# Twenty-three Strassen pairs instead of twenty-two, and a new order of visits, in a weight-gradient matmul

## The chip, the cores and the metric

The kernel runs on one core of a Trainium2 chip. The time is device microseconds of one execution; the figure for a kernel is the median of several runs. A profile is one execution taken by the hardware profiler, and its times run from the start of its own span.

The engines have short names in the profile: PE is TensorE, which multiplies matrices, and PEld its loading of weights; DVE is VectorE; ACT is ScalarE; POOL is GpSimd, which here only issues loads; SP is SyncE, which issues stores. SBUF is the on-chip memory, PSUM the small memory into which TensorE writes, in eight banks.

## What is computed

```python
batch, m, k, n = 16, 512, 1024, 768
grad_weight = np.einsum('bmk,bmn->kn', input, grad_output)   # float32
```

The batch and the rows of a batch are summed over alike, so this is one product: the transpose of an 8192 x 1024 matrix X with an 8192 x 768 matrix G. The output is 1024 x 768.

## The kernel before

**Blocks and units.** The 8192 rows are cut into 64 blocks of 128 rows. Two blocks make a unit, 32 units in all. Loads convert from float32 to bf16 on the way. The output has four quarters: A (left columns of X, left columns of G), B (left, right), C (right, left) and D (right, right), each 512 x 384. A quarter is four tiles of 128 x 384, one PSUM bank each. So an item costs TensorE four matmuls per product, with 128 x 128 weights from X and 384 moving columns from G.

**Plain items and pairs.** `LOADS` has a letter for each unit. "s" makes two plain items: each of A, B, C and D gets one product from each block, 4 x 4 x 2 = 32 matmuls per unit. "P" makes one pair: the two blocks count as a 2 x 2 arrangement, and Strassen's scheme takes seven products in place of eight, 28 matmuls. Two of the seven are summed straight into A and D; five go into sums of their own, called m, n, o, p and q. The price is six additions on VectorE per pair, three on G and three on X (`sum_g1` to `sum_g3`, `sum_x1` to `sum_x3`, lines 132 to 155). `sum_g3` and `sum_x3` change the loaded block in place. At the end m to q are added to or subtracted from A to D by `share` (line 190), in the order of `SHARES`: t1 stands for the tile rows of A and B that take m and o, l1 for those of C and D, and so on.

**Visits.** PSUM has eight banks, hence room for two of the nine sums at a time (two slots of four banks). `ORDER` is a list of visits, written out by hand. `A17:4!2,1,1,1` reads: go to sum A and multiply all its items up to number 17; `:4` says how many of the four banks ScalarE carries; `!` says that the sum is closed at the end of the visit, and the four numbers how many VectorE fillers (pair sums first, then shares) stand ahead of each bank's eviction. A number ahead of the letter (`5D23`) is how many fillers stand ahead of the visit. A sum is summed on through several visits as long as it stays open.

**What opening and closing cost.** When a sum is closed, each bank is evicted to its accumulator in SBUF (`acc` for A to D, `macc` for m to q). ScalarE evicts the last so many banks by a plain copy (line 300) and must then reload them from SBUF at the next opening (line 267) before TensorE adds on; VectorE evicts the others by adding the bank to the accumulator (line 304, or a copy at line 302 the first time), with no reload. `C20:0+n` opens C from n's accumulator in place of its own (line 274; with a minus sign, line 272), and `share` then leaves that part out.

**Queues.** PE, DVE, ACT and POOL each run their instructions in the order in which the code emits them. POOL issues all loads at the start of its list: for units 2 to 31 first G, then X (lines 107 and 108), held back only by buffers (14 pairs) and by the eight loads that may be in flight. The first blocks come in float32 over SP and ACT, in halves, and are cast by VectorE and ScalarE (`round_by`, lines 210 to 216 and 361 to 367). The last visit has its last tile split into 256 and 128 columns, so that its store can start sooner (lines 329 to 347).

Of the kernel before, what the change touches and what calls it, by code (L numbers as in the profile page):

```python
# [8 lines left out]

P = 128  # L10

LOADS = "ssssssssPPPPPPPPPPPPPPPPPPPPPPss"

ORDER = (
    "C1:4!0,0,0,0 A1 D2:3!0,0,0,0 A2!0,0,0,0 B2:1 C3:3 C4!0,0,0,0 B4!0,0,0,0 A3 A4!0,0,0,0 D4 "
    "B6:3!0,0,0,0 D6 C6:1 C8!0,0,0,0 A8!0,0,0,0 D8 B7:2!0,0,0,0 D10!0,0,0,0 B10:2!0,0,0,0 "
    "A10!0,0,0,0 B12:2!0,0,0,0 C10 A12 A14!0,0,0,0 D14:2!0,0,0,0 C16!0,2,1,1 B16:4!1,0,1,1 D16 "
    "A17:4!2,1,1,1 q2:3!0,1,1,1 m2:3!0,0,0,0 D17 p3:3!2,0,1,1 D18!0,0,0,0 n3:4!0,0,0,2 o3:4 "  # L20
    "3A20:3!3,0,0,1 o4 q5:3!2,0,1,2 m5!0,0,0,0 o6!1,1,0,1 n6!1,0,0,0 p6:4 D20:3 D21 5D23 "
    "3p8!1,1,1,0 A24:2!1,0,1,1 m8:1 2m9!1,0,0,0 D25!0,0,0,1 o9 2o10!2,0,0,0 q9:4 q10!3,1,0,0 "
    "p11!1,0,0,0 n11:4 5o12:4!3,0,1,0 m12:1 n12!5,0,0,0 m13!0,0,0,0 A27 q13:4!4,0,2,0 A30!1,0,0,1 "
    "D29:3 p12:4 1p15 D30 6p16!2,1,0,0 D31!0,0,0,1 o16!2,0,1,0 n17:3!0,1,2,2 m16 A32:3!4,0,0,1 "
    "m18!0,0,0,0 q18 4D35:4!3,0,2,1 q20!0,0,0,0 p19:3 o17:4 3p21 o21 6o22!2,1,0,0 p22!0,0,0,0 A36 "
    "q22:4!3,1,0,1 1A39 m22:4!1,1,1,1 A40 n22:3!1,2,0,1 A42!2,0,0,0 C20:0+n!0,0,0,1 B20:4!0,1,2,2 "
    "D42!2,0,0,0 "
).split()


SHARES = (
    "l20 l21 l22 l23 t20 t21 t22 t23 t10 t11 t12 t13 t30 t31 t32 t33 l10 l11 l12 l13 l30 l31 l32 "
    "l33 "
).split()

WARMUP = [512] * 10 + [128] * 2
# [7 lines left out]
def kernel(  # L44
# [55 lines left out]
    xg = []  # L100
    for u, kind in enumerate(LOADS):
        pool = pairs if u else head
# [299 lines left out]
```

## Time and profile before

| | |
|---|---|
| time, median of 3 runs | 164.0 us (163.97 to 164.2) |
| profiled execution | 164.11 us, span 162.3 us |
| TensorE clock granted | 1.00 |
| PE, PEld busy | 158.0, 93.6 us |
| DVE, ACT, POOL busy | 134.1, 96.4, 34.7 us |
| moved by DMA | 33.4 MB |

A line of the groups or of the timeline reads: line in the code, engine, operation, output <- input, shape, count, then busy time, the mean of one, and idle time of the engine ahead of it with what ended it. In the timeline the first two numbers are start and length of a run of like instructions. An instruction on VectorE or ScalarE overlaps the next one by a little, so the distance of starts, not the length of one, says what it costs in a row.

### The profile page before, as it was taken

What the parts mean: (1) busy time and instruction counts of PE and PEld (TensorE: products, weight loads), DVE (VectorE), ACT (ScalarE), POOL (GpSimd) and SP (SyncE); (2) the same over time, 40 slices, a digit from 0 to 9 for tenths busy, and PEclk for the clock granted to TensorE, in tenths of its full rate; (3) what the DMA queues carried; (4) which work ended last, traced back from release to release, by engine and by line L of the source; (5) the groups of instructions that cost most, each with busy time, mean ns of one, the idle gap of its engine ahead of it and who ended that gap; (6) DMA issues with size and microseconds to landing.
All of it is one profiled execution on the core that took longest, in us unless ns stands there. A gap on an engine that the chain in (4) does not pass through costs nothing.

```text
span 162.3 us, 2773 instructions
## 1 busy us (share of the span) xinstructions
PE 158.0 (97%) x955; PEld 93.6 (58%) x955; DVE 134.1 (83%) x276; ACT 96.4 (59%) x225; POOL 34.7 (21%) x69
## 2 busy tenths in 40 slices
PE   8999999999999999999999999999999999999992
PEld 2456556665666665665665666666666666666661
DVE  0467367945978999998899999989999979999982
ACT  3764716415388667735475779809573907987620
POOL 7442222222222221222222222222212100000000
PEclk9999999999999999999999999999999999999999
DMA  5999999999999999999999999999999999800974
GB/s 170 293 213 213 212 212 216 214 212 212 214 213 213 212 212 214 212 211 213 212 213 217 211 213 215 212 211 216 211 212 214 211 212 212 172 4 2 346 276 156
DMA packets 12398, 33.40 MB, mean 206 GB/s; under 512 B 1376, under 2 KB 4192, under 8 KB 12384
## 3 DMA queue, kind: packets, MB, share of 16 engines
q0 software_dynamic: 9360, 28.64, 89.2%
q1 hardware_dynamic: 2592, 3.47, 6.1%
q10 hardware_dynamic: 432, 1.11, 1.9%
q8 instruction: 7, 0.11, 0.3%
q14 instruction: 7, 0.06, 0.1%
HBM read 58.72 MB, written 3.15 MB: 381 GB/s over the span
## 4 chain that ended last, share of the span: by engine, by line
PE 92%; DMA 4%; DVE 1%; issue 1%; ACT 0%; ACTq 0%; POOLq 0%
PE bank L286 92%; DMA gp<-in_grad_output_dram 4%; PE bank L337 0%; DVE acc L345 0%; DVE acc L304 0%; ACT bank L267 0%; ACTq L267 0%; POOLq L386 0%
## 5 line engine op out<-in xcount | busy, mean ns | idle before, releaser
L286 PEld LDWEIGHTS <-xp 128*128 128x128 bf16 x665 | 64.9, 98 | 44.6 <-issue 0.7
L286 PE MATMUL bank<-gp,xp 128*128 128x384 bf16 x492 | 85.2, 327 | 0.4 <-ACT bank L267 0.2
L300 ACT COPY macc<-bank 128x384 f32<-128x384 f32 x67 | 29.1, 494 | 27.6 <-PE bank L286 27.2
L304 DVE TENSOR_TENSOR acc<-bank,acc 128x384 f32<-128x384 f32 x62 | 31.5, 550 | 12.7 <-PE bank L286 12.2
L286 PEld LDWEIGHTS <-xe 128*128 128x128 bf16 x264 | 25.8, 98 | 17.1
L300 ACT COPY acc<-bank 128x384 f32<-128x384 f32 x53 | 23.5, 486 | 19.0 <-PE bank L286 18.7
L286 PE MATMUL bank<-ge,xp 128*128 128x384 bf16 x173 | 32.1, 326 | 0.0
L286 PE MATMUL bank<-gp,xe 128*128 128x384 bf16 x176 | 30.8, 326 | 0.0
L108 POOL DMA_DIRECT2D xp<-in_input_dram x30 | 15.9, 530 | 52.6 <-DMA xp<-in_input_dram 30.4
L267 ACT COPY bank<-acc 128x384 f32<-128x384 f32 x45 | 20.3, 487 | 8.9 <-DVE acc L304 7.9
L107 POOL DMA_DIRECT2D gp<-in_grad_output_dram x30 | 16.0, 532 | 38.1 <-DMA gp<-in_grad_output_dram 21.0
L267 ACT COPY bank<-macc 128x384 f32<-128x384 f32 x50 | 21.9, 515 | 0.1
L304 DVE TENSOR_TENSOR macc<-bank,macc 128x384 f32<-128x384 f32 x38 | 19.0, 550 | 1.3 <-PE bank L286 1.2
L146 DVE TENSOR_TENSOR xe<-xp 128x1024 bf16<-128x1024 bf16 x22 | 15.0, 684 | 2.8 <-DMA xp<-in_input_dram 2.8
L190 DVE TENSOR_TENSOR acc<-acc,macc 128x768 f32<-128x768 f32 (+1 forms) x24 | 16.4, 750 | 0.1
L286 PE MATMUL bank<-ge,xe 128*128 128x384 bf16 x88 | 15.6, 326 | 0.0
L155 DVE TENSOR_TENSOR xp<-xp 128x1024 bf16<-128x1024 bf16 x22 | 15.0, 682 | 0.0
L132 DVE TENSOR_TENSOR ge<-gp 128x768 bf16<-128x768 bf16 x22 | 12.1, 550 | 0.3 <-DMA gp<-in_grad_output_dram 0.2
L141 DVE TENSOR_TENSOR gp<-gp 128x768 bf16<-128x768 bf16 x22 | 12.1, 549 | 0.0
L150 DVE TENSOR_TENSOR xe<-xp 128x512 bf16<-128x512 bf16 x22 | 9.2, 416 | 0.0
L136 DVE TENSOR_TENSOR ge<-gp 128x384 bf16<-128x384 bf16 x22 | 7.7, 349 | 0.0
L90 PE MATMUL bank<-const-bfloat16-1.0 128*128 128x512 bf16 (+1 forms) x12 | 4.6, 577 | 0.8 <-PEq L386 0.8
(19 smaller groups left out, 20.7 us busy)
## 6 DMA issues: line engine op xcount, KB each, us to landing
xp<-in_input_dram POOLq DMA_DIRECT2D x30, 512.0 KB, 16.8
gp<-in_grad_output_dram POOLq DMA_DIRECT2D x30, 384.0 KB, 16.7
out_dram<-acc SPq DMA_DIRECT2D x15, 192.0 KB, 2.1
xf<-in_input_dram ACTq DMA_DIRECT2D x2, 512.0 KB, 5.1
gp<-in_grad_output_dram POOLq DMA_DIRECT2D x3, 192.0 KB, 6.7
xp<-in_input_dram POOLq DMA_DIRECT2D x2, 256.0 KB, 8.0
gf<-in_grad_output_dram SPq DMA_DIRECT2D x2, 192.0 KB, 4.5
out_dram<-acc SPq DMA_DIRECT2D x1, 128.0 KB, 1.7
```

Source lines behind the costliest of these rows:

```text
L107: nc.gpsimd.dma_start(out=gp, in_=G[rows, :].rearrange("(p m) n -> p m n", m=2))
L108: nc.gpsimd.dma_start(out=xp, in_=X[rows, :].rearrange("(p m) k -> p m k", m=2))
L132: nc.vector.tensor_add(out=ge[:, 0:2, :], in0=g[:, :, 0, :], in1=g[:, :, 1, :])
L141: nc.vector.tensor_sub(out=g[:, 1:3, :], in0=g[:, 1:3, :], in1=g[:, 3::-3, :])
L146: nc.vector.tensor_add(out=xe[:, 0:2, :].rearrange("p a k -> p (a k)"), in0=xp[:, 0, :], in1=xp[:, 1, :])
L150: nc.vector.tensor_add(out=extra[i][0][:, 2, :], in0=xp[:, 0, 0:KH], in1=xp[:, 1, KH:K])
L155: nc.vector.tensor_sub(out=x[:, 1:3, :], in0=x[:, 1:3, :], in1=x[:, 0::3, :])
L190: op(out=dst, in0=dst, in1=src)
L267: nc.scalar.copy(out=bank, in_=sum_of(p, q))
L286: nc.tensor.matmul(bank, stat, mov, start=opening and j == 0 and not carried, stop=close and j == len(items_now) - 1, skip_group_check=car ...
L300: nc.scalar.copy(out=dst, in_=bank)
L304: nc.vector.tensor_add(out=dst, in0=bank, in1=dst)
```

## The change

Unit 7 becomes a pair: fourteen plain blocks at the front and four at the end remain around 23 pairs. The last four names of t3, `t30` to `t33`, leave `SHARES`, whose order changes too; the sum q enters A by opening it, negated (`A34:0-q`). And `ORDER` is a new list: it starts with A, D, C and B, and ends with a visit to D of the same length as before. Nothing else in the code changes; its lines stand one higher.

```diff
-LOADS = "ssssssssPPPPPPPPPPPPPPPPPPPPPPss"
+LOADS = "sssssssPPPPPPPPPPPPPPPPPPPPPPPss"
 ORDER = (
-    "C1:4!0,0,0,0 A1 D2:3!0,0,0,0 A2!0,0,0,0 B2:1 C3:3 C4!0,0,0,0 B4!0,0,0,0 A3 A4!0,0,0,0 D4 "
-    "B6:3!0,0,0,0 D6 C6:1 C8!0,0,0,0 A8!0,0,0,0 D8 B7:2!0,0,0,0 D10!0,0,0,0 B10:2!0,0,0,0 "
-    "A10!0,0,0,0 B12:2!0,0,0,0 C10 A12 A14!0,0,0,0 D14:2!0,0,0,0 C16!0,2,1,1 B16:4!1,0,1,1 D16 "
...
-    "q22:4!3,1,0,1 1A39 m22:4!1,1,1,1 A40 n22:3!1,2,0,1 A42!2,0,0,0 C20:0+n!0,0,0,1 B20:4!0,1,2,2 "
-    "D42!2,0,0,0 "
+    "A1:3!0,0,0,0 D1:1 C2:4!0,0,0,0 B2:2!0,0,0,0 D3!0,0,0,0 A2 B4:1!0,0,0,0 A3 C4:2!0,0,0,0 "
+    "A4!0,0,0,0 D5 D6!0,0,0,0 C6 B5 B6 B7 B8 C8!0,0,0,0 A8:1!0,0,0,0 D10:2!0,0,0,0 B10!0,0,0,0 "
+    "A10:4 A12!0,0,0,0 C11!0,0,0,0 B14:2!0,2,0,0 C14:1!0,0,0,0 2D14:2 2A15:2!3,0,0,1 o2:4!2,0,0,0 "
...
+    "p8 A20:4 3A22!3,0,1,0 p9!1,0,0,1 m9:3 D23:4!0,2,2,1 q10!1,0,1,0 m10 4o10:4 m11!0,1,0,0 "
...
+    "8q18!0,0,0,1 o18 n16:4 4n19!0,2,0,3 D32 o20!1,0,1,1 D33 q20:2!1,0,0,0 D34!1,0,0,2 1m20:2 "
+    "p17:4 m21!4,0,0,0 1p20 p22 3q22:2 3p23!2,0,0,0 q23!0,0,0,0 o23!0,0,0,0 A34:0-q m23:4!4,1,0,0 "
+    "A37 n23:4!0,3,1,0 A41!1,0,1,0 C15:0+p C18!0,1,0,0 B18:4!0,0,1,2 D41!4,0,1,0 "
 ).split()
 SHARES = (
-    "l20 l21 l22 l23 t20 t21 t22 t23 t10 t11 t12 t13 t30 t31 t32 t33 l10 l11 l12 l13 l30 l31 l32 "
-    "l33 "
+    "t20 t21 t22 t23 t10 t11 t12 t13 l10 l11 l12 l13 l20 l21 l22 l23 l30 l31 l32 l33 "
 ).split()
```

## The prediction

> **What bounds the kernel now.** I read the busy shares and slices first, then the chain of waits, then the groups by line, then the timelines of TensorE, ScalarE and VectorE.
>
> ```profile
> PE 158.0 (97%) x955; PEld 93.6 (58%) x955; DVE 134.1 (83%) x276; ACT 96.4 (59%) x225; POOL 34.7 (21%) x69
> ...
> PE   8999999999999999999999999999999999999992
> ...
> DVE  0467367945978999998899999989999979999982
> ...
> DMA  5999999999999999999999999999999999800974
> ...
> PE 92%; DMA 4%; DVE 1%; issue 1%; ACT 0%; ACTq 0%; POOLq 0%
> ...
> L286 PE MATMUL bank<-gp,xp 128*128 128x384 bf16 x492 | 85.2, 327 | 0.4 <-ACT bank L267 0.2
> ```
>
> TensorE is the bound: 92% of the chain is L286. "327" is the latency of a matmul, not its price. The price is the distance of starts, from its timeline:
>
> ```profile
> 34.74 3.09 PE L286 MATMUL bank<-gp,xp 128*128 128x384 bf16 x18
> 38.01 7.31 PE L286 MATMUL bank<-gp,xp 128*128 128x384 bf16 x44 [0.18 <-ACT bank L267]
> ...
> 56.85 2.11 PE L286 MATMUL bank<-gp,xp 128*128 128x384 bf16 x12
> 58.80 2.11 PE L286 MATMUL bank<-ge,xp 128*128 128x384 bf16 x12
> ```
>
> Twelve matmuls take 58.80 - 56.85 = 1.95 us, so 162.5 ns each. The kernel has 929 at L286 and 7 whole ones' worth at L337: 936 x 0.1625 = 152.1 us. The first starts at 5.50, so without a wait the stream would end near 157.6; it ends near 159.05 by starts. Only some 1.4 us is idle or slow: about 0.45 in the first four, which start 0.3 us apart, 0.29 before the tenth (the second block's landing at 7.67), 0.17 at 20.7 (a landing), and 0.35 in the lines above: the eighteenth starts at 34.74 + 17 x 0.1625 = 37.50, the next at 38.01. There ScalarE started a reload 0.38 us after VectorE released it (the wait at L267 below). The rest is under 0.2 us.
>
> VectorE is the second. A pair's six sums cost the distance between the first sums of two pairs with nothing between them, 93.90 - 91.15 = 2.75 us; an eviction of four in 1.94 us costs (1.94 - 0.55)/3, or 0.47 us:
>
> ```profile
> 37.47 0.90 ACT L267 COPY bank<-acc 128x384 f32<-128x384 f32 x2 [4.22 <-DVE acc L304]
> ...
> 68.09 1.94 DVE L304 TENSOR_TENSOR macc<-bank,macc 128x384 f32<-128x384 f32 x4
> ...
> 91.15 0.55 DVE L132 TENSOR_TENSOR ge<-gp 128x768 bf16<-128x768 bf16 x1
> ...
> 93.90 0.55 DVE L132 TENSOR_TENSOR ge<-gp 128x768 bf16<-128x768 bf16 x1
> ```
>
> The DMA row is full until 140 us because loads run ahead on their own pace (one unit per 4.3 us); TensorE is stopped by a landing only at the two places named.
>
> **What the Trainium skill says.** "TensorE: Matmul & The Clock Gate", section "Wait — 56ns, not 53.3ns?", gives warm starts N/2.4 + 2.5 ns apart: 162.5 ns for 384 columns, exactly what the trace has. Its section "What's actually happening" says the array runs at half rate until it has been busy for some 3.4 us; the first four matmuls, 0.3 us apart, agree. "VectorE: DVE Perf Modes", section "The perf-mode tier table (the rule you actually need)", has tensor_tensor at twice the rate for bf16 in SBUF and at single rate with PSUM: here 768 bf16 take 550 ns and 384 f32 from PSUM take 550 ns too. So evictions cannot be had cheaper by moving them about on VectorE.
>
> **The change part by part.** Counts are from the two instruction orders.
>
> (1) Unit 7 becomes a pair: 28 matmuls instead of 32. **-4 x 0.1625 = -0.65 us** on TensorE, all of it on the path. VectorE gains 2.75 us of sums and may start them when unit 7 lands (36.3 us) rather than unit 8 (40.6).
>
> (2) Shares: the four one-sided subtractions t3 go (4 x 0.47 = -1.9 us on VectorE). In their place A34 opens its banks with the negated q by four ScalarE multiplies at L272. Not seen in the trace; at least a plain copy L274 (0.41 us apart), at most twice that. They fall at 136 to 138 us, beside o23's twelve matmuls (1.95 us) on the other banks: 0 on the path, at most 0.3.
>
> (3) Order: VectorE's evictions rise from 111 to 122 (+11 x 0.47 = +5.2 us). ScalarE's fall from 120 to 117 and its reloads and openings from 99 to 98: about -1.5 us. VectorE in sum +2.75 - 1.9 + 5.2 = **+6.0 us**. That is not on the path while sums stay ahead of use. Before, from 40.7 to 135.5, VectorE has 22 x 2.75 + 56 x 0.47 = 86.8 us in 94.8. After, from 36.3 to about 135.5 (the last pair's landing at 133.9 is the same) it has 23 x 2.75 + 68 x 0.47 = 95.2 in 99.2. Its slack falls from 8.0 to 4.0 us.
>
> (4) Start: A1, D1, C2 instead of C1, A1, D2. A1 needs the columns cast first, so it can start at 5.3, not 5.5. D1 needs the right half of the first gradient block, which is cast from 6.46 to 6.82. Four matmuls, a wait, four more end at 7.5; in both orders the tenth waits for 7.67. **0**, between -0.05 and +0.2.
>
> (5) Loads and end: POOL issues the same 65 DMAs in the same order, SP and ACT the same loads and stores, the last visit is again seven items with a split last bank. **0**; a pair buffer freed late would have to be late by more than the 16.7 us that a load is in flight. The 3.1 us from last matmul to end stay.
>
> (6) Waits that go and come. The 0.35 at 37.5 belongs to D14's reload, released late by an A14 eviction; that pair of visits is gone. How far the late start of ScalarE would recur I cannot see: 0 to -0.35, I take -0.2. New waits, worked on the same clock (7.72 us at the tenth matmul, 0.1625 each): A10:4 is matmul 144, wanted at 29.9 after 0.2 of earlier waits. Its bank 3 was left by D10 at 28.7, ScalarE evicts it from 28.8 and reloads four banks from 29.2 every 0.413, ready at 29.75, 30.16, 30.57 and 30.99; a two-item visit takes a bank every 0.325, at 29.87, 30.20, 30.52 and 30.85. Wait 0.14. The same sum gives 0.15 at A20:4, 0.17 at C4:2 and some 0.1 at q20:2. Sums: 8q18 is matmul 656, reached at 113.6. VectorE must have done 17 pairs (46.7), four sums of the 18th (1.8) and 55 evictions (25.8), 74.3 us from 36.3: ready at 110.6 plus its own waits. In the whole stretch before, those on TensorE were 2.7 us and those on landings 3.0. So ready about 113.3 to 114: some 0.1 here and 0.1 at 4n19. Together **+0.6**, less 0.15 for the small waits of before that go with their visits: +0.45. Bounds: 0 if each reload starts a little earlier than I reckon, +1.2 if VectorE is 1 us later.
>
> Sum: -0.65 - 0.2 + 0.45 = **-0.4 us**. The profiled execution took 164.1, the median of three is 164.0 (163.97 to 164.2). 164.0 - 0.4 = **163.6**. Less than 0.2% (0.33 us) is about what this measurement can't tell from no change.
>
> **The rivals.**
> Full gain: both kinds of waits vanish: -0.65 - 0.2: 163.15. For it: searched margins could be as wide as 0.1 us. Against it: every two-item visit with four reloads loses 3 x 0.088 us unless it starts ahead. Chance 0.10.
> New waits eat it: +0.7 to +0.9 of waits against -0.65 and no gain from the old: 164.0 to 164.2. For it: evictions in all rise from 231 to 239, each a bank to be emptied in time. 0.23. This is also the case in which the change doesn't do what it says, a longer lead.
> Slower: VectorE becomes the bound between 60 and 120 us. Its in-order queue mixes sums with evictions that wait on TensorE; when these waits exceed the 2.9 us that I allow up to matmul 656, each further microsecond delays the sums, and TensorE by as much. Waits of 4.1 us (half again the old 2.7) give 1.2. With -0.65, -0.2 and +0.25 for the reloads that is +0.6, so 164.6; from 3.5 us on it is slower than before. For it: slack halved. Against it: VectorE, running behind the landings, no longer waits for them. 0.17.
>
> **How the numbers follow.** The forecast -0.4 has 0.50, its own range 163.3 to 163.95. Faster by over 0.2%: 0.40 of the forecast's case and the full gain's 0.10: 0.50. Within: 0.10 of the first and 0.20 of the second rival: 0.30. Slower: 0.03 of the second and 0.17 of the third: 0.20. The range 163.2 to 164.5 leaves out about half the full gain and over half the slower case, some 0.15.
>
> **What would show it.** Right: 925 matmuls at L285, starts still 162.5 ns apart, the wait of 0.2 us near 38 us gone, small waits on ScalarE's bank reloads at 14-16, 30-31 and 72 us, VectorE's busy sum near 140 us, and the last matmul near 158.8. Wrong: VectorE waiting less than 2 us between 36 and 113 us (then the full gain), or waits of TensorE's weight loads on xe, xp or of its matmuls on ge by over 0.5 us together (then the third rival); a clock below 1.0 or loads ending later than 142.5 would upset all of it.

## The result, and the profile after

The changed kernel takes **163.57 us** (median of 6 runs, 163.39 to 163.7), the kernel before 163.99 (6 runs, 163.84 to 164.2): ratio **0.9972**, 95% interval 0.9959 to 0.9985. The profiled execution took 163.7 us, its span 161.9 (before 162.3), at a granted clock of 1.00. The gain is 0.42 us, and the changed kernel has four matmuls less (x951 in place of x955), which are worth 0.65.

The page of the changed kernel, with the rows that were shown of before:

```profile
PE 157.1 (97%) x951; PEld 92.7 (57%) x951; DVE 139.6 (86%) x289; ACT 94.6 (58%) x221; POOL 34.6 (21%) x69
...
PE   8799999999999999999999999999999999999992
...
DVE  0557947469979999999989999999998999999992
...
DMA  5999999999999999999999999999999999902675
...
PE 93%; DMA 3%; DVE 1%; SPq 0%; issue 0%
...
L285 PE MATMUL bank<-gp,xp 128*128 128x384 bf16 x468 | 80.9, 326 | 1.0 <-DVE gp L206 1.0
```

TensorE is the bound as before, and VectorE is busier by 5.5 us. New are the 7 in the second slice of PE and, in the last row, one idle time of 1.0 us, ended by VectorE's cast of gp (L206). The chain of waits of the changed kernel tells the same (start, length, what):

```profile
1.17 5.52 DMA gf<-in_grad_output_dram
...
6.71 0.37 DVE gp L206
...
7.12 150.51 PE bank L285 x921
157.64 0.78 PE bank L336 x7
```

Once TensorE has the cast half block at 7.12, it is a single piece to the end. In the chain of before it starts at 7.72, after a landing, and is broken twice, by a landing at 20.75 and by the late reload at 38.01:

```profile
1.23 6.45 DMA gp<-in_grad_output_dram
...
7.72 13.03 PE bank L286 x79
...
38.01 120.05 PE bank L286 x737
```

"One piece" doesn't mean that nothing waits: the chain doesn't break for waits below some 0.1 us. I took them from the timeline of TensorE, as the distance of two starts beyond 162.5 ns. The lines of the changed kernel that hold such a wait:

```profile
7.12 35.12 PE L285 MATMUL bank<-gp,xp 128*128 128x384 bf16 x214 [0.96 <-DVE gp L206]
...
71.09 2.89 PE L285 MATMUL bank<-ge,xp 128*128 128x384 bf16 x16
...
74.46 2.81 PE L285 MATMUL bank<-ge,xe 128*128 128x384 bf16 x16
...
112.27 2.87 PE L285 MATMUL bank<-gp,xe 128*128 128x384 bf16 x16
...
115.63 4.79 PE L285 MATMUL bank<-gp,xe 128*128 128x384 bf16 x28
```

Sixteen matmuls without a wait take 15 x 0.1625 + 0.33 = 2.76 us, 28 take 4.71 and 214 take 34.94. So these lines hold 0.18, 0.13, 0.05, 0.11 and 0.08 us. From the tenth matmul to the last, all such waits sum to:

| | before | changed |
|---|---|---|
| start of the tenth matmul | 7.72 | 7.93 |
| waits after it | 0.68 | 0.69 |
| start of the last matmul | 158.99 | 158.58 |

So the account of these two executions is **-0.65 for the four matmuls, +0.21 for a later start, +0.02 for the waits: -0.42 us**. The 0.68 of before are a landing (0.17 at 20.4 us), the late reload (0.345 at 37.5) and small ones. The 0.69 after are all small: 0.066 at 15.1 us (C4), 0.13 at 30.4 to 30.8 (A10), 0.063 at 43.7 (X of unit 8, landed at 43.89), 0.13 at 71.6 to 71.9 (A20), 0.045 and 0.054 at 75.0 and 84.1, 0.097 at 113.6 (8q18), 0.065 at 118.4 (4n19), 0.013 at 124.3 (q20), and 0.03 in single hundredths.

### The profile page after: what moved, and what is told of

Same layout as the page of the kernel before. It is cut to its first block, busy times and chain, and to the rows that moved or that the text cites. A ratio compares the mean times of both kernels' runs of the same rounds, so it can differ in the third digit from the quotient of the medians.

```text
span 161.9 us, 2755 instructions
## 1 busy us (share of the span) xinstructions
PE 157.1 (97%) x951; PEld 92.7 (57%) x951; DVE 139.6 (86%) x289; ACT 94.6 (58%) x221; POOL 34.6 (21%) x69
## 4 chain that ended last, share of the span: by engine, by line
PE 93%; DMA 3%; DVE 1%; SPq 0%; issue 0%
PE bank L285 93%; DMA gf<-in_grad_output_dram 3%; PE bank L336 0%; DVE acc L344 0%; SPq L81 0%; DVE gp L206 0%
## 5 line engine op out<-in xcount | busy, mean ns | idle before, releaser
L285 PEld LDWEIGHTS <-xp 128*128 128x128 bf16 x649 | 63.3, 98 | 43.6 <-issue 1.5
L285 PE MATMUL bank<-gp,xp 128*128 128x384 bf16 x468 | 80.9, 326 | 1.0 <-DVE gp L206 1.0
L299 ACT COPY macc<-bank 128x384 f32<-128x384 f32 x73 | 31.5, 493 | 25.0 <-PE bank L285 24.9
L303 DVE TENSOR_TENSOR acc<-bank,acc 128x384 f32<-128x384 f32 x69 | 34.7, 551 | 8.7 <-PE bank L285 8.3
L285 PE MATMUL bank<-gp,xe 128*128 128x384 bf16 x184 | 32.4, 326 | 0.0
L266 ACT COPY bank<-macc 128x384 f32<-128x384 f32 x56 | 25.3, 503 | 8.0 <-DVE macc L303 6.9
L299 ACT COPY acc<-bank 128x384 f32<-128x384 f32 x44 | 19.5, 486 | 15.4 <-PE bank L285 15.3
L107 POOL DMA_DIRECT2D xp<-in_input_dram x30 | 15.9, 530 | 53.1 <-DMA xp<-in_input_dram 29.8
L106 POOL DMA_DIRECT2D gp<-in_grad_output_dram x30 | 15.9, 531 | 37.5 <-DMA gp<-in_grad_output_dram 14.8
L303 DVE TENSOR_TENSOR macc<-bank,macc 128x384 f32<-128x384 f32 x44 | 22.5, 552 | 1.5 <-PE bank L285 1.2
L266 ACT COPY bank<-acc 128x384 f32<-128x384 f32 x34 | 15.2, 492 | 8.6 <-DVE acc L303 8.5
L189 DVE TENSOR_TENSOR acc<-acc,macc 128x768 f32<-128x768 f32 (+1 forms) x20 | 14.6, 791 | 0.0
```

Source lines behind the costliest of these rows:

```text
L106: nc.gpsimd.dma_start(out=gp, in_=G[rows, :].rearrange("(p m) n -> p m n", m=2))
L107: nc.gpsimd.dma_start(out=xp, in_=X[rows, :].rearrange("(p m) k -> p m k", m=2))
L189: op(out=dst, in0=dst, in1=src)
L266: nc.scalar.copy(out=bank, in_=sum_of(p, q))
L285: nc.tensor.matmul(bank, stat, mov, start=opening and j == 0 and not carried, stop=close and j == len(items_now) - 1, skip_group_check=car ...
L299: nc.scalar.copy(out=dst, in_=bank)
```

## The experiments

Each asks what decides one term of that account. Ratios are against runs of the kernel before on the same chip in the same session; the chip is not the same in all sections. The theory that I held is the prediction's: fewer matmuls, less a few small waits at places that can be named, VectorE behind but not the bound.

### The changed kernel again

The same code a second time, to see what in the profile is the kernel's and what is one execution's.

> The changed kernel itself, as the yardstick for the others on the same chip. Its trace gave the account to be tested: four matmuls fewer -0.65 us, the start +0.21 (fifth matmul at 7.12 because the right half of the first gradient block landed at 6.69), waits after the tenth matmul 0.70 before and 0.69 now. If the start's wait is a landing that jumps about, the landing lies between 6.4 and 6.7 and the time at 163.4 to 163.7, 0.3 to 0.6 us under before.

Measured: 163.54 us (163.43 to 165.12, 8 runs, seven of them below 163.71), before 163.95; ratio 0.9987 with an interval of 0.9965 to 1.001, which has the one run of 165.12 in it. The half block of G whose cast opened TensorE at 6.71 in the first profile landed earlier here. VectorE's and TensorE's timelines of this run:

```profile
6.25 0.35 DVE L206 CAST gp<-gf 128x384 bf16<-128x384 f32 x1
```

```profile
6.65 3.60 PE L285 MATMUL bank<-gp,xp 128*128 128x384 bf16 x20 [0.37 <-DVE gp L206]
```

The fifth matmul starts at 6.65 in place of 7.12, the tenth at 7.65 in place of 7.93: the start costs nothing this time. The data lay there at 5.97 (I had expected 6.4 to 6.7), and the cast waited only for an eviction ahead of it on VectorE. So the loss at the start is that of one landing, which came at 5.97 once and at 6.69 once.

But 0.17 of the 0.28 us gained are lost again at matmul 62, in the visit D5, which wants X of unit 2. From the timeline of the weight loads of this run:

```profile
16.32 1.74 PEld L285 LDWEIGHTS <-xp 128*128 128x128 bf16 x12 [0.39 <-DMA xp<-in_input_dram]
```

That load landed at 16.29 here. In the first profile it was there at 16.24, and TensorE, late from the start, came only at 16.45. The same wait, 0.17 to 0.20 us, stands in the profiles of four edits below (A10, A20, the six additions, the second sums). So the new order wants this landing before it comes, and a late start hides it: the term of the start and that of the waits are not independent. The waits after the tenth matmul sum to 0.83 here; those at 30, 71.6, 84, 113.6 and 118.4 us return.

### The pairs without the new order

Twenty-three pairs with the order of before, its items numbered anew and six fillers set ahead of C14:

```diff
-    "A1:3!0,0,0,0 D1:1 C2:4!0,0,0,0 B2:2!0,0,0,0 D3!0,0,0,0 A2 B4:1!0,0,0,0 A3 C4:2!0,0,0,0 "
+    "C1:4!0,0,0,0 A1 D2:3!0,0,0,0 A2!0,0,0,0 B2:1 C3:3 C4!0,0,0,0 B4!0,0,0,0 A3 A4!0,0,0,0 D4 "
...
+    "A10!0,0,0,0 B12:2!0,0,0,0 C10 A12 A14!0,0,0,0 D14:2!0,0,0,0 6C14!0,2,1,1 B14:4!1,0,1,1 D15 "
+    "A16:4!2,1,1,1 q3:3!0,1,1,1 m3:3!0,0,0,0 D16 p4:3!2,0,1,1 D17!0,0,0,0 n4:4!0,0,0,2 o4:4 "
...
```

> Twenty-three pairs visited in the old order: the same visits with items renumbered, six fillers more ahead of C14, old shares. Theory 1 (the pair's 0.65 us is only to be had with an order that leaves VectorE room): VectorE gets 2.75 us of sums more with its old slack of 8 us spread in the wrong places, and TensorE waits on sums or reloads by some 2 us more: slower than before by 1 to 2.5 us, about 165.5. Rival (the pair brings the gain, the order is neutral): 163.4, and no waits on VectorE.

Measured: **166.2 us** (165.88 to 166.47), ratio 1.0131, interval 1.0115 to 1.0146. The 0.65 us of the extra pair are gone, and over 2 us on top. TensorE's timeline of this run where it happens:

```profile
43.23 0.49 PE L286 MATMUL bank<-ge,xp 128*128 128x384 bf16 x2
43.90 0.32 PE L286 MATMUL bank<-ge,xp 128*128 128x384 bf16 x1 [0.17 <-DVE acc L304]
44.96 0.48 PE L286 MATMUL bank<-ge,xp 128*128 128x384 bf16 x2 [0.74 <-DVE acc L304]
45.90 1.31 PE L286 MATMUL bank<-ge,xp 128*128 128x384 bf16 x7 [0.45 <-DVE xp L155]
...
48.47 1.80 PE L286 MATMUL bank<-gp,xe 128*128 128x384 bf16 x10 [0.93 <-DVE xe L146]
```

Four waits, 2.97 us in all between 40 and 60 us; in the 102 us from 60 to 162 only 0.13. TensorE waits for evictions (acc L304) and for sums (xp L155, xe L146) by turns. The queue of VectorE in this run shows why:

```profile
40.56 0.68 DVE L155 TENSOR_TENSOR xp<-xp 128x1024 bf16<-128x1024 bf16 x1
41.16 0.55 DVE L304 TENSOR_TENSOR acc<-bank,acc 128x384 f32<-128x384 f32 x1
41.63 0.55 DVE L132 TENSOR_TENSOR ge<-gp 128x768 bf16<-128x768 bf16 x1
...
42.36 0.55 DVE L304 TENSOR_TENSOR acc<-bank,acc 128x384 f32<-128x384 f32 x1
...
45.16 0.68 DVE L155 TENSOR_TENSOR xp<-xp 128x1024 bf16<-128x1024 bf16 x1
...
47.72 0.69 DVE L146 TENSOR_TENSOR xe<-xp 128x1024 bf16<-128x1024 bf16 x1 [0.67 <-DMA xp<-in_input_dram]
```

Up to 47 us it works back to back, and C14's evictions stand behind one or two sums each: D15, which takes over C14's banks, gets them only when sums that are wanted later are done. The third wait is for the last sum of the second pair (unit 8). The fourth and longest, 1.10 us, is for the first X sum of the third pair, and there VectorE itself waited: X of unit 9 landed at 47.70. So this order asks for unit 9 before it is loaded.

The changed kernel doesn't come to the pairs later. From its TensorE and VectorE timelines:

```profile
42.09 0.33 PE L285 MATMUL bank<-ge,xp 128*128 128x384 bf16 x1
...
48.98 2.11 PE L285 MATMUL bank<-gp,xe 128*128 128x384 bf16 x12
```

```profile
44.86 0.68 DVE L154 TENSOR_TENSOR xp<-xp 128x1024 bf16<-128x1024 bf16 x1
```

Its first product of a pair is in A15, at matmul 219 (42.09 us); with the old order it is D15, at matmul 225 (43.23). The last sum of the second pair is done at 45.54, against 45.84 here. What differs is what TensorE wants next. The old order wants that last sum at matmul 230, in A16, and unit 9 at matmul 239, in q3; with twenty-two pairs the same visits come to unit 9 only at matmul 262, for a plain unit 7 has 32 matmuls there and a pair only the 8 of A and D. In the same way only B14's 8 matmuls lie between C14's end and D15, where there were 16. The new order sets o2, m2, D15, n2 and D16, products of the first two pairs, ahead of q3, and comes to unit 9 at matmul 263 (q3 starts at 48.98). So **with the old order of visits the extra pair's 0.65 us is lost, since TensorE asks for C14's banks and for the second and third pair before VectorE and the loads have them ready**. The loss with this order is measured; its causes are read from the timelines, and no run changes one of them alone. What fails first is the step from plain items to pairs, not VectorE's slack at 60 to 120 us, on which my slower case rested.

### The start of before, put ahead of the new order

The first nine visits of before (C1 first), then D4 D5 D6, and from C6 the new order:

```diff
-    "A1:3!0,0,0,0 D1:1 C2:4!0,0,0,0 B2:2!0,0,0,0 D3!0,0,0,0 A2 B4:1!0,0,0,0 A3 C4:2!0,0,0,0 "
-    "A4!0,0,0,0 D5 D6!0,0,0,0 C6 B5 B6 B7 B8 C8!0,0,0,0 A8:1!0,0,0,0 D10:2!0,0,0,0 B10!0,0,0,0 "
+    "C1:4!0,0,0,0 A1 D2:3!0,0,0,0 A2!0,0,0,0 B2:1 C3:3 C4!0,0,0,0 B4!0,0,0,0 A3 A4!0,0,0,0 D4 D5 "
+    "D6!0,0,0,0 C6 B5 B6 B7 B8 C8!0,0,0,0 A8:1!0,0,0,0 D10:2!0,0,0,0 B10!0,0,0,0 A10:4 "
...
```

> The changed kernel with the first nine visits of the kernel before (C1, A1, D2 ... A4, then D4, D5, D6 as three visits). The right half of the first gradient block is wanted 4 matmuls later. Theory 1 (the start costs 0.2 and all of it reaches the end): tenth matmul at 7.72 in place of 7.9, end 0.2 us earlier, about 163.35. Rival (VectorE sets the pace later on): the 0.2 us is given back at the sums of 114 and 118 us, where the waits of 0.10 and 0.07 grow to 0.2 or more, and the time is that of the changed kernel within 0.05.

Measured: 164.78 us (164.5 to 165.14, 5 runs), ratio 1.0052, interval 1.0039 to 1.0064. Neither theory had that. TensorE's timeline of this run:

```profile
7.92 13.03 PE L285 MATMUL bank<-gp,xp 128*128 128x384 bf16 x79 [0.78 <-DMA gp<-in_grad_output_dram]
...
PE bank L285 <- DMA xp<-in_input_dram: 1.4, 1, 1.4
```

The last line is from its waits (line, what it waited for, us in all, times, longest). The tenth matmul is at 7.92, so here too a landing decides. The whole loss is **one wait of 1.52 us** after the 79 matmuls of the first line: B7 needs X of unit 3, and of the sixteen parts of that landing fifteen were there by 20.92 us and one at 22.27. At 20.24 an instruction load of 16 KB, by all signs TensorE's, had begun; it took 0.95 us.

A second form wants unit 3 only at matmul 96 (A6 ahead of C6), with ScalarE's shares and the sums fitted up to 42 us:

```diff
-    "A4!0,0,0,0 D5 D6!0,0,0,0 C6 B5 B6 B7 B8 C8!0,0,0,0 A8:1!0,0,0,0 D10:2!0,0,0,0 B10!0,0,0,0 "
-    "A10:4 A12!0,0,0,0 C11!0,0,0,0 B14:2!0,2,0,0 C14:1!0,0,0,0 2D14:2 2A15:2!3,0,0,1 o2:4!2,0,0,0 "
...
+    "D6!0,0,0,0 A6:1!0,0,0,0 C6:1 B5 B6 B7 B8 C8!0,0,0,0 A8!0,0,0,0 D10:1!0,0,0,0 B10!0,0,0,0 "
+    "A10:3 A12!0,0,0,0 C11!0,0,0,0 B14:1!0,1,0,1 C14!1,0,0,0 2D14:3 1A15:4!2,2,0,0 o2:4!2,0,0,0 "
```

> The old start again (C1, A1, D2 ... A4), now with a visit A6 ahead of C6, so that unit 3 is first wanted at matmul 96, at 21.9 us, and not at 88 (20.6), and with ScalarE's shares and the sums around it fitted between 18 and 42 us (A8, D10, A10, B14, C14, D14, A15). In the first run of the old start TensorE waited 1.52 us at matmul 87 for unit 3's X, whose last sixteenth landed at 22.27 while fifteen lay at 20.92 or before; a 16 KB load of instructions had started at 20.24. Theory 1 (that one landing is the whole loss): the wait is 0.4 or less, time 163.4 to 163.8. Rival (the old start costs 1 us in some other way): 164.6 or more.

Measured: 163.59 us (163.34 to 163.81, 17 runs), ratio 0.9978, interval 0.997 to 0.9985; the tenth matmul at 7.67, waits 0.80. That is the time of the changed kernel: **the new start in itself gains nothing and costs nothing**, though this form has other visits changed as well, and unit 3 landed at 20.66 here.

A third form is the first one without the two 128-column matmuls at the end of the warm-up, which should put the instruction load at another place:

```diff
-WARMUP = [512] * 10 + [128] * 2
+WARMUP = [512] * 10
```

> The old start as in the first run of it, with the two last warm-up matmuls (128 columns, no part of the result) taken out and nothing else changed. TensorE's own 16 KB load of instructions came at about its 199th instruction in each kernel; with four instructions (two weight loads, two matmuls) fewer ahead it comes two matmuls, 0.33 us, later, at 20.57 in place of 20.24. Theory 1 (that load held up one sixteenth of unit 3's X): the landing comes at 20.7 to 20.9, the wait of 1.52 us at matmul 87 falls to 0.3 or less, time 163.4 to 163.7. Rival (the old start itself costs 1 us): 164.6 or more, with the wait as before.

Measured: 22 runs in two groups, 8 at 163.36 to 163.82 and 14 at 164.8 to 165.24 (median of all 164.82, ratio 1.0026, interval 1.0006 to 1.0045). The instruction load didn't move as I expected: it came at 19.95. The profiled execution took 164.86; its TensorE timeline:

```profile
22.03 1.15 PE L285 MATMUL bank<-gp,xp 128*128 128x384 bf16 x6 [1.48 <-DMA xp<-in_input_dram]
```

Again one sixteenth of X of unit 3 landed late, at 21.98 against 20.51 for the others. So, by its times, one and the same program has this wait of 1.5 us in some executions and not in others. The eight shorter runs have the old start too, and the time of the changed kernel.

That the instruction load causes the wait isn't shown: the repeat of the changed kernel has that load at 20.32 and the second form at 20.08, and unit 3 was on time in both. But the landings of all fourteen profiles point at it. Up to about 20.7 us the last part of a load comes at most 0.17 us after the fifteenth, save for X of unit 3 in the two profiles with the long wait. With the next load, G of unit 4, the last part is 0.46 to 1.02 us late in every one of them. And in those two profiles the instruction load had begun 0.68 and 0.56 us before the fifteenth part of unit 3's X was there, in the other twelve at most 0.45 us before.

The changed kernel wants unit 3 at matmul 89, 20.8 us, nearly as early. Its one run of 165.12 among 14 would fit, as would two runs of 165.6 and one of 164.89 in edits of it below, each some 1.6 above its median; I have no profile of these runs.

### Two opening visits with fewer reloads

A10:4 means four banks carried by ScalarE, hence four reloads in a row. The changed kernel's ScalarE timeline has them as reckoned, from 29.26 us:

```profile
29.26 1.72 ACT L266 COPY bank<-acc 128x384 f32<-128x384 f32 x4
```

Here ScalarE carries two, and VectorE evicts the other two:

```diff
-    "A10:4 A12!0,0,0,0 C11!0,0,0,0 B14:2!0,2,0,0 C14:1!0,0,0,0 2D14:2 2A15:2!3,0,0,1 o2:4!2,0,0,0 "
+    "A10:2 A12!0,0,0,0 C11!0,0,0,0 B14:2!0,2,0,0 C14:1!0,0,0,0 2D14:2 2A15:2!3,0,0,1 o2:4!2,0,0,0 "
```

> A10:4 becomes A10:2, so ScalarE reloads two banks and VectorE evicts two in place of four by ScalarE, at 30 us, where VectorE has no sums yet. Theory 1 (reload every 0.413 us against a bank used every 0.325): the gaps at 30.4 and 30.8 us (0.04 and 0.09) go, end 0.13 earlier. Rival (other waits take their place): gaps elsewhere grow and the time stays.

Measured: 163.35 us (163.24 to 163.64), ratio 0.9967, interval 0.9955 to 0.998. Its TensorE timeline:

```profile
5.21 36.91 PE L285 MATMUL bank<-gp,xp 128*128 128x384 bf16 x218
```

From 20 to 40 us there is no wait at all (0.13 before the edit), the others stay where the repeat had them. The gain of 0.2 us on the median is within what single runs scatter; that the two waits belong to A10's reloads is shown by their going.

The same edit at A20, where VectorE has less room:

```diff
-    "p8 A20:4 3A22!3,0,1,0 p9!1,0,0,1 m9:3 D23:4!0,2,2,1 q10!1,0,1,0 m10 4o10:4 m11!0,1,0,0 "
+    "p8 A20:2 3A22!3,0,1,0 p9!1,0,0,1 m9:3 D23:4!0,2,2,1 q10!1,0,1,0 m10 4o10:4 m11!0,1,0,0 "
```

> A20:4 becomes A20:2 at 71 us: as at A10, ScalarE reloads two banks fewer and VectorE evicts two more at A22, 0.94 us. Theory 1 (VectorE has no room here, other than at 30 us): the gaps at 71.6 and 71.9 us (0.04 and 0.09) go, but VectorE's next sums come 0.9 us later and TensorE waits for them between 72 and 120 us: 0.3 to 0.6 us slower than the changed kernel, about 164.0. Rival (the reloads are the cost, VectorE has room): 0.13 us faster, 163.4.

Measured: 164.03 us (163.95 to 164.27 in 20 of 22 runs, 165.6 in two), ratio 1.0014, interval 1.0001 to 1.0027: 0.5 **slower** than the changed kernel. Its TensorE timeline:

```profile
70.90 2.76 PE L285 MATMUL bank<-ge,xp 128*128 128x384 bf16 x16
...
74.15 0.65 PE L285 MATMUL bank<-ge,xe 128*128 128x384 bf16 x3
75.33 2.29 PE L285 MATMUL bank<-ge,xe 128*128 128x384 bf16 x13 [0.53 <-DVE xe L149]
```

The sixteen matmuls that took 2.89 take 2.76, so A20's two waits are gone; but two evictions more on VectorE put the next sum x2 0.9 us later, and TensorE waits 0.69 for it. The four reloads were the cheaper choice here: a wait of 0.13 stood in place of one of 0.69.

### How near is VectorE to being the bound?

Six additions of 0.47 us on a spare tile, spread over 60 to 110 us, once in the kernel before and once in the changed one. They touch nothing that is stored.

```diff
+EXTRA = (41, 49, 55, 64, 72, 77)
...
+        if n in EXTRA:
+            nc.vector.tensor_add(out=spare, in0=spare, in1=spare)
```

(In the kernel before the visits are 38, 44, 51, 57, 63 and 71, at the same times.)

> The kernel before with six additions of 384 float32 on a scratch tile put into VectorE's queue, one every 10 us between 60 and 110 us, 0.47 us each, 2.8 us in all. Nothing depends on them. Theory 1 (VectorE runs close to TensorE in both kernels, with some slack left by its waits for landings): about half of the 2.8 us comes through, +1.0 to +1.6 us. Rival (TensorE alone is the bound and VectorE's 83% leave room): +0.0 to +0.3.

> The changed kernel with the same six additions at the same times. Theory 1 (the change has used up VectorE's slack, 8.0 us down to 4.0, and it waits for no landing any more): most of the 2.8 us comes through, 2.0 to 2.6 us over the changed kernel, so about 165.8, slower than before with the same additions. Rival (slack as large as before): as much as in the kernel before, 1.0 to 1.6.

Measured: in the kernel before 165.62 us against 163.92, **+1.70**, ratio 1.0099 (1.0083 to 1.0116); in the changed kernel 165.86, ratio 1.0109 (1.0093 to 1.0125), **+2.3** over its 163.54 (from another chip, where the kernel before stands at 163.95). The first is a little more than I expected, the second is inside. Of 2.8 us added, 60% and 82% came through, so the kernel before could hide 1.1 us and the changed one 0.5. The waits of the weight loads, first in the kernel before with the additions, then in the changed one with them (line, what it waited for, us in all, times, longest):

```profile
PEld L288 <- DVE xp L157: 0.9, 2, 0.5
...
PEld L288 <- DVE xe L148: 0.5, 1, 0.5
PEld L288 <- DVE xe L152: 0.2, 1, 0.2
```

```profile
PEld L287 <- DVE xe L147: 1.7, 3, 0.8
...
PEld L287 <- DVE xp L156: 0.9, 3, 0.5
PEld L287 <- DVE xe L151: 0.9, 2, 0.4
```

1.6 us on sums in the one, 3.5 in the other; the changed kernel without additions has 1.3 us on the same three kinds of sums (0.8, 0.3, 0.2; part of it is hidden behind the matmul before).

The opposite: the changed kernel without the second sums `sum_g2` and `sum_x2`, 13.9 us by distances of starts (the busy sum below falls by less, for an instruction with nothing close behind it counts at its whole length). m multiplies the first sums in their place, so its value isn't that of the reference.

```diff
-        nc.vector.tensor_add(out=extra[i][1][:, 2, :], in0=gp[:, 0, 0:NH], in1=gp[:, 1, NH:N])
+        pass
...
-            "m": lambda: (xe[:, 2, k], ge[:, 2, :]),
+            "m": lambda: (xe[:, 0, k], ge[:, 0, :]),
```

> The changed kernel without sum_g2 and sum_x2: VectorE loses 23 x (0.27 + 0.335) = 13.9 us of work, and the m products take the first sum of each side in place of the third, so that the output is another one. Theory 1 (of the 0.69 us of waits, some 0.25 are VectorE's, at 84, 114 and 118 us, the others ScalarE's reloads): these three gaps go, the others stay: 163.3. Rival A (VectorE sets the pace all along): 1 us or more faster. Rival B (the three gaps are hidden by others): no change from 163.55.

Measured: 163.27 us (163.14 to 163.49 in 21 of 22 runs, 164.89 in one), ratio 0.996, interval 0.9949 to 0.997: **0.27 below the changed kernel**. From its page, and from its TensorE timeline:

```profile
PE 156.4 (97%) x951; PEld 92.8 (58%) x951; DVE 130.1 (81%) x243; ACT 94.9 (59%) x221; POOL 34.8 (22%) x69
```

```profile
70.81 2.89 PE L285 MATMUL bank<-ge,xp 128*128 128x384 bf16 x16
```

The waits at 84, 113.6 and 118.4 us are gone, from 80 to 120 nothing is left; A20's 0.13 in the first line stays, as do those at 15, 30 and 75 and the landing at 16. The three waits that went are 0.22 us, and the intervals of the two ratios overlap a little, so the quarter of a microsecond rests on the timeline and the median together. This is what late sums cost the changed kernel; the waits that stay are, by their places, reloads, as the prediction had it, and landings, which it had not.

### Two other orders for twenty-three pairs

If small waits are all that is left, an order with wider margins at just those places should gain them. I laid out two. The first cuts visits into shorter ones and puts fillers ahead of them:

```diff
...
+    "A1:4!0,0,0,0 D1:1 B2:4!0,0,0,0 C2:3!0,0,0,0 D2 D3!0,0,0,0 A2 B4!0,0,0,0 A3 A4!0,0,0,0 "
+    "C4:4!0,0,0,0 D4 D5 D6!0,0,0,0 C5 C6 B5 B6 B7 C8!0,0,0,0 A8!0,0,0,0 B8 B9 D7 B10!0,0,0,0 D8 "
+    "D9 D10!0,0,0,0 A9:1 A10 A11 C9:2 C10 C11!0,0,0,0 A12!0,0,0,0 1C14!0,0,0,0 1B13:3 B14!0,3,0,0 "
...
```

> Twenty-three pairs in a further order, fitted by hand sums of the durations measured so that each bank's reload and each sum ends ahead of its use: long visits cut into single items, their evictions and sums moved; 108 VectorE evictions in place of 122 hold its queue shorter. Same matmuls, same start (A, D, then B). Theory 1 (what is left of waits after the tenth matmul, 0.69 us, lies in the order alone): 0.1 to 0.2 left, time 163.0 to 163.2, faster than both kernels. Rival (the waits are a floor that moves about): 163.5.

Measured: 163.27 us (163.2 to 163.51), ratio 0.9963, interval 0.9951 to 0.9976, just above the 163.0 to 163.2 that I expected. The expectation is wrong in one count: it says 108 VectorE evictions, and the trace has 72 + 42 + 4 + 1 = 119 against 122. The waits after the tenth matmul fell to 0.36, 0.24 of them new, at 43.6 to 44.4 us, at the step from plain items to pairs.

The second takes more evictions off VectorE, here the whole list for whoever wants to build it:

```diff
+    "A1:4!0,0,0,0 D1:2 C2:4!0,0,0,0 B2:1!0,0,0,0 D2 D3!0,0,0,0 A2 B4:2!0,0,0,0 A3 C4:2!0,0,0,0 "
+    "A4!0,0,0,0 D5:2 D6!0,0,0,0 B5 B6 C6:2 C8!0,0,0,0 B7 A5 B8 A8!0,0,0,0 D10:4!0,0,0,0 B9 "
+    "B10!0,0,0,0 A9:1 A10 A12!0,0,0,0 C10 C12!0,0,0,0 C13 1C14!0,0,1,0 1B14:3!0,1,1,2 D14:2 "
+    "A15:4!0,2,1,0 o2:4!0,0,2,0 D15 m2:3!1,2,0,0 D16!0,0,1,1 n2:3!0,0,0,1 q3:4!2,0,1,1 1A16 p1:4 "
+    "4p4!0,0,0,0 A18!0,0,0,0 m3:2 1m4 o5:4!0,0,2,0 m5!1,0,1,0 D19:1 2q6:4!3,1,0,0 1D20!0,0,0,0 p5 "
+    "p6 1o7:2!0,0,1,0 1n5:1 n7!3,0,0,2 1p8 A20:3 2A22!1,0,0,0 p9!1,1,1,0 2m8:2 m9 2D23:4!1,1,0,0 "
+    "q10!1,0,0,0 m10 o9:4 5o11!1,0,0,1 m11!0,0,1,0 n8 n9 2n10 n11 1n12!0,0,0,0 p10:3 p12!0,2,0,1 "
+    "1A23 A24 1A25 2o13:4!0,1,0,0 A27!0,0,1,0 q12:3 4D27:2 q14!2,2,1,0 2D28 m15:3!0,0,1,0 "
+    "3p16:2!0,0,0,1 D30!0,1,1,0 A30:1!1,0,1,1 1q15 q16 o17:4 3q18!2,0,0,1 1o18 3n17:3 n19!1,1,0,1 "
+    "D32 2o20!0,0,0,0 3D33 q20:1!1,0,1,0 D34!0,0,0,0 1m20:3 3p17:4 m21!0,1,2,1 p18 1p19 1p20 "
+    "q21:2 q22 p21 1p22 1p23!0,0,0,0 1q23!2,0,0,1 o22 o23!0,0,0,0 A34:0-q m22:4 m23!1,2,0,2 A35 "
+    "A36 A37 n23:4!0,0,0,1 A41!3,0,0,0 C15:0+p 1C16 C17 1C18!1,0,0,1 B15:4 1B17 B18!0,1,0,1 "
+    "1D41!2,0,0,0 "
```

> A second order of that sort, with A, D, then C at the start as in the changed kernel. Theory 1: 163.0 to 163.2. Rival: 163.5.

Measured: **163.14 us** (162.94 to 163.33), ratio **0.9952**, interval 0.9939 to 0.9966, the lowest median of this study; its interval overlaps that of the changed kernel (0.9959 to 0.9985). From its page and its chain:

```profile
PE 156.3 (97%) x951; PEld 92.7 (57%) x951; DVE 135.5 (84%) x281; ACT 100.4 (62%) x235; POOL 34.6 (21%) x69
```

```profile
7.47 149.46 PE bank L287 x916
156.93 0.78 PE bank L338 x7
```

VectorE is at 135.5 us in place of 139.6, ScalarE at 100.4 in place of 94.6, the tenth matmul at 7.47, and the waits after it sum to 0.45: 0.25 at 12.3 to 15.9 us and 0.20 at 65. The seven pieces of the split last tile start at 156.93, 0.71 us sooner than in the changed kernel (157.64): 0.24 from the waits (0.69 to 0.45), 0.46 from the start (7.93 to 7.47), which the repeat of the changed kernel showed to vary with a landing. Of that, 0.2 is given back in the last stores (from the last evictions' start to the end of the span 3.7 us in place of 3.5), so the spans stand 0.5 apart and the medians 0.43.

## Why the prediction was right, and where it wasn't

The forecast of 163.6 us and the time of 163.57 agree, and the largest term, the four matmuls, is right. But in the profiled execution **two terms were off and cancelled**: the start cost 0.21 us in place of 0, the waits 0.02 in place of 0.25. In the repeat they fall otherwise, -0.07 for the start and +0.15 for the waits. That the sum is met to 0.03 us is luck.

- **Step 1, -0.65 us: right.** The starts are still 162.5 ns apart and four are gone.
- **Step 2, shares and the four multiplies: right.** ScalarE's timeline of the changed kernel has them at 137.16, and the distance of their starts is (1.78 - 0.54)/3 = 0.41 us with 0.54 for the last one's length, the lower of my two bounds. No matmul of A34 waits.

```profile
137.16 1.78 ACT L271 ACTIVATE bank<-macc 128x384 f32<-128x384 f32 x4
```

- **Step 3, VectorE +6.0 us: nearly right.** The busy sum rose by 5.5 us, the evictions to 122. ScalarE fell by 1.8 where I had 1.5.
- **Step 4, start 0 (-0.05 to +0.2): this step failed in the profiled execution.** It was +0.21. I took the cast of the right half from before, 6.46 to 6.82; here it ran from 6.71 to 7.07, since its landing came at 6.69, and in the repeat from 6.25. The bound was drawn from a single landing time. What the step should have said is that the new order makes the fifth matmul wait for a landing that moves by 0.7 us. In the repeat, and in the old start put ahead of the new order (tenth at 7.92, 7.67 and 7.52 in its three forms), it came out either way.
- **The slow first matmuls, half right.** In the kernel before they are 0.3 us apart, as at half rate. But this held until 6.43 us, 5.65 us after the first warm-up matmul at 0.78, so the 3.4 us of work that the prediction cites doesn't by itself give the moment. In the changed kernel only the second is late (starts 5.21, 5.52, 5.68).
- **Step 5, loads and end 0: right for the end, not for the loads.** The last landing is at 142.48 (142.54 before), and last matmul start to end of span is 3.3 us in both. But what the new order wants of the loads wasn't reckoned: X of unit 2 at matmul 62 costs 0.17 to 0.20 us in five of the six profiles of this order, at the place of the 0.17 for unit 3 before.
- **Step 6, waits +0.25 net: this term was mis-sized, it measured +0.02.** Of the old waits I counted 0.35 as gone (0.2 of the late reload, 0.15 of the small ones); all 0.68 went, but in the repeat a landing brought 0.17 back. Of the new ones I had 0.6 at six places, where my own six figures add up to 0.76; those six measured 0.50 (0.13 for 0.14 at A10, 0.13 for 0.15 at A20, 0.10 for 0.1 at 8q18, 0.065 for 0.1 at 4n19, 0.066 for 0.17 at C4, 0.013 for 0.1 at q20), and 0.16 came at three places that I hadn't named (43.7, 75.0 and 84.1). With 0.76 the forecast would have been -0.24, so this slip helped it. That A10's and A20's belong to reloads and those at 84 to 118 to sums is shown by the edits that removed each.
- **The arithmetic behind 8q18 held, with two errors in it.** I had the sum ready at 110.6 us plus 2.9 of waits. VectorE's timeline has x1 of pair 18 from 113.09 to 113.77:

```profile
113.09 0.68 DVE L145 TENSOR_TENSOR xe<-xp 128x1024 bf16<-128x1024 bf16 x1
```

  But its waits on TensorE from 36.3 to 113.7 us were only 1.8 (0.8 + 0.7 + 0.3, below), those on landings 0.5. So some 0.9 us more of work than my count stood ahead of it.

```profile
DVE macc L301 <- PE bank L285: 0.8, 1, 0.8
DVE macc L303 <- PE bank L285: 0.7, 2, 0.4
DVE acc L303 <- PE bank L285: 0.3, 1, 0.3
```

  I had named less than 2 us of waiting as the sign of the full gain. That sign was no good: the waits on TensorE were below 2 us (2.3 with the landings), and the full gain didn't come.
- **The rivals.** That new waits eat the gain fell: the waits after the tenth matmul are as long as before (0.15 longer in the repeat). That VectorE is the bound is a real limit, but the point from which it decides wasn't reached: the changed kernel could hide another 0.5 us, and 2.8 us more made it 2.3 slower. With its margin my reckoned slack had the right sign (8.0 to 4.0 us) and no more; what an added microsecond costs is set by the sums that are late one at a time. The place where the extra pair hurts is another than that rival's: with the old order it is the step into the pairs at 43 to 48 us.

**Open:** whether the instruction load is what makes one sixteenth of unit 3's X land 1.35 to 1.47 us late in some executions (no run moved it alone), and whether the changed kernel's run of 165.12 is the same. No run has a new order with twenty-two pairs, so what a better order gives without the extra pair isn't shown. Also open is why ScalarE started a reload 0.38 us after its release at 37.1 us in the kernel before. The runs with the old order have that gap again, 0.35 at 37.5; the kernels without this pair of visits don't have it. An instruction load of 8 KB lies near it, at 35.83, which I didn't try to move.

## What to carry to other kernels

When one engine works back to back, price a change by the distances of its starts, and keep the waits in a list by place and cause: here nine small waits at named places made up the waits of the changed kernel, and five of them could be edited away. Terms that follow one another in time are not independent: a late start hides a landing that comes after it. Where the work on a second engine grows, look first at the step where it begins, not at its mean slack: the same extra pair gained 0.4 us with an order that comes to the third pair at matmul 263 and lost 2.2 with one that comes to it at matmul 239, before it was loaded. And read a term that hangs on one landing from several profiles, for a single profile gives a bound that is too narrow.

## What the runs showed of the hardware

- The instruction loads appear as DMA traffic among the data: 16 KB each, which I take for TensorE's, at about 20.3, 42, 62.5 and 83 us, 0.95 us for the one at 20.24.
- After the one at 20 us, one part in sixteen of the load that lands at about 23 us (G of unit 4) comes 0.46 to 1.02 us after the other fifteen in all fourteen profiles; in the loads ahead of the instruction load the last part is at most 0.17 us behind.
- One part in sixteen of a 512 KB load can come 1.35 to 1.47 us after the other fifteen (22.27 against 20.92, 21.98 against 20.51 in two profiles); by the times, in 14 of 22 executions of one program and not in the other 8.
- The same first load landed at 5.97 and at 6.69 us in two profiles of the same program, and TensorE's fifth matmul started at 6.65 and at 7.12.
